# Rotary embedding on one core: loads and stores from two DMA queues, or from one queue in a written order

## The chip, the core and the metric

The kernel runs on one core of a Trainium2 chip. The metric is device time in microseconds, the median of three runs. A profiled execution gives the trace from which all other times here come.

## The reference

```
x: (8, 2048, 16, 64) float32; cos, sin: (2048, 32) float32
x1, x2 = x[..., :32], x[..., 32:]
out1 = x1 * cos - x2 * sin        # cos, sin per sequence position,
out2 = x1 * sin + x2 * cos        # the same for all batches and heads
out  = concat([out1, out2], -1)
```

Each element is read once and written once: 67.1 MB in, 67.1 MB out, three vector operations on each.

## The kernel before

A batch's 2048 positions lie on 128 partitions, 16 consecutive positions on each. A piece is half of that: 8 positions, 128 partitions x 8192 floats, 4 MB. There are 16 pieces, and `buf` has room for 5 of them; piece p uses place p mod 5, is rotated in place and is stored from there. So the load of piece p + 5 has to wait until piece p is stored.

At the start SyncE issues the two tables and the first piece in three parts (L101 to L105), then pieces 1 to 4 (L106, `load` at L52). ScalarE copies the tables into PSUM (`sin_p` with both signs, `cos_p`; L108 to L110). ScalarE then does nothing but issue stores (`store` at L55).

`rotate` works on half a piece (4 positions, 128 x 4096). VectorE multiplies the half-swapped piece by sin into `v` (L80) and the piece by cos in place (L93); GpSimd adds `v` to it (L99). `v` has two buffers, so VectorE can be at most two halves ahead of GpSimd. In piece 15 a part of the adds stays on VectorE, with `w` in PSUM (L87, L96), and the store is cut in three. The order of VectorE's work is pinned by `in_order`.

Loads are in SyncE's DMA queue, stores in ScalarE's; each queue is in order in itself. When both have work, packets of 32 KB (one partition's row of a piece) from the two alternate on each of the 16 DMA engines. Nothing ties the order of one queue to that of the other except the data: a store waits for GpSimd (and VectorE in piece 15), a load for the store that frees its place, the arithmetic for its load. Below, load 5 and store 5 are short for those of piece 5.

Of the kernel before, what the change touches and what calls it, by code (L numbers as in the profile page):

```python
# [1 line left out]

# [4 lines left out]


@with_exitstack  # L10
def kernel(
    ctx: ExitStack,
    tc: tile.TileContext,
    x: bass.AP,
    cos: bass.AP,
    sin: bass.AP,
    out: bass.AP,
):
    nc = tc.nc
    f32 = mybir.dt.float32  # L20

    B, S, H, D = x.shape
    Dh = D // 2
    P = nc.NUM_PARTITIONS
    J = S // P
    R = 8
    C = 4
    HALVES = J // R
    NP = B * HALVES
    NBUF = 5  # L30

    const_pool = ctx.enter_context(tc.tile_pool(name="rope_const", bufs=1))
    io_pool = ctx.enter_context(tc.tile_pool(name="rope_io", bufs=1))
    tmp_pool = ctx.enter_context(tc.tile_pool(name="rope_tmp", bufs=2))
    ps_pool = ctx.enter_context(tc.tile_pool(name="rope_ps", bufs=1, space=bass.MemoryType.PSUM))
    psv_pool = ctx.enter_context(tc.tile_pool(name="rope_psv", bufs=1, space=bass.MemoryType.PSUM))

    sin_f = const_pool.tile([P, J, Dh], f32)
    cos_f = const_pool.tile([P, J, Dh], f32)
    sin_p = ps_pool.tile([P, J, D], f32)  # L40
    cos_p = ps_pool.tile([P, J, Dh], f32)
    buf = io_pool.tile([P, NBUF, R, H, D], f32)

    def rows(t, p, r0, r1):
        b, j0 = p // HALVES, (p % HALVES) * R
        return t[b].rearrange("(p j) h d -> p j (h d)", j=J)[:, j0 + r0 : j0 + r1, :].rearrange("p j f -> p (j f)")

    def flat(t):
        return t.rearrange("p j h d -> p (j h d)")

    def load(p, r0=0, r1=R):
        nc.sync.dma_start(out=flat(buf[:, p % NBUF, r0:r1, :, :]), in_=rows(x, p, r0, r1))  # L52

    def store(p, r0=0, r1=R):
        nc.scalar.dma_start(out=rows(out, p, r0, r1), in_=flat(buf[:, p % NBUF, r0:r1, :, :]))  # L55

    order = []

    def in_order(op):
        if order:  # L60
            tc.add_manual_dep(
                op.ins,
                order[-1].ins.name,
                mybir.DependencyInfo(mybir.DependencyClass.NoSync, mybir.DependencyReason.DATA),
                reason="order of the vector engine",
            )
        order.append(op)

    def rotate(p, r0, r1, on_vector=0):
        n = r1 - r0  # L70
        j0 = (p % HALVES) * R + r0
        js = slice(j0, j0 + n)
        xt = buf[:, p % NBUF, r0:r1, :, :]
        rev = xt.rearrange("p j h (e d) -> p j h e d", e=2)[:, :, :, ::-1, :]
        sin_b = sin_p[:, js, :].rearrange("p j (e d) -> p j e d", e=2).unsqueeze(2).to_broadcast([P, n, H, 2, Dh])
        cos_b = cos_p[:, js, :].unsqueeze(2).to_broadcast([P, n, 2 * H, Dh])
        m = n - on_vector
        if m:
            v = tmp_pool.tile([P, C, H, D], f32)
            in_order(nc.vector.tensor_mul(  # L80
                out=v[:, 0:m, :, :].rearrange("p j h (e d) -> p j h e d", e=2),
                in0=rev[:, 0:m, :, :, :],
                in1=sin_b[:, 0:m, :, :, :],
            ))
        if on_vector:
            w = psv_pool.tile([P, 2, H, D], f32)
            in_order(nc.vector.tensor_mul(  # L87
                out=w[:, 0:on_vector, :, :].rearrange("p j h (e d) -> p j h e d", e=2),
                in0=rev[:, m:n, :, :, :],
                in1=sin_b[:, m:n, :, :, :],  # L90
            ))
        xw = xt.rearrange("p j h (e d) -> p j (h e) d", d=Dh)
        in_order(nc.vector.tensor_mul(out=xw, in0=xw, in1=cos_b))  # L93
        if on_vector:
            xa = flat(xt[:, m:n, :, :])
            in_order(nc.vector.tensor_add(out=xa, in0=xa, in1=flat(w[:, 0:on_vector, :, :])))  # L96
        if m:
            xa = flat(xt[:, 0:m, :, :])
            nc.gpsimd.tensor_add(out=xa, in0=xa, in1=flat(v[:, 0:m, :, :]))  # L99

    nc.sync.dma_start(out=sin_f, in_=sin.rearrange("(p j) d -> p j d", j=J))  # L101
    load(0, 0, 2)
    nc.sync.dma_start(out=cos_f, in_=cos.rearrange("(p j) d -> p j d", j=J))
    load(0, 2, 4)
    load(0, 4, R)  # L105
    for p in range(1, NBUF):  # L106
        load(p)
    nc.scalar.copy(out=sin_p[:, :, Dh:D], in_=sin_f)  # L108
    nc.scalar.mul(out=sin_p[:, :, 0:Dh], in_=sin_f, mul=-1.0)  # L109
    nc.scalar.copy(out=cos_p, in_=cos_f)  # L110
    for p in range(NP):
        if p == 0:
            rotate(p, 0, 2)
            rotate(p, 2, 4)
            rotate(p, 4, 8)
            store(p)
        elif p == NP - 1:
            rotate(p, 0, 4, 1)
            store(p, 0, 4)
            rotate(p, 4, 6, 1)  # L120
            store(p, 4, 6)
            rotate(p, 6, 8, 2)
            store(p, 6, 8)
        else:
            rotate(p, 0, 4)
            rotate(p, 4, 8)
            store(p)
        if p + NBUF < NP:
            load(p + NBUF)


# [1 line left out]
_INS = ['x', 'cos', 'sin']  # L133
_OUTS = [((8, 2048, 16, 64), 'float32')]


# [23 lines left out]
```

## Time and profile before

| | |
|---|---|
| median of 3 runs | 318.86 us (318.46 to 319.0) |
| the profiled execution | 318.49 us, of which the span is 316.7 us |
| VectorE busy | 287.5 us (91%), 73 instructions |
| GpSimd busy | 274.8 us (87%), 37 instructions |
| ScalarE busy | 3.1 us |
| loads, queue 1 | 67.63 MB, 50.0% of the 16 DMA engines' span |
| stores, queue 10 | 67.11 MB, 49.1% |
| a 4 MB load or store, issue to landing | 31.4 us (median) |

An engine's busy time is what it spends in instructions; issuing a DMA isn't counted. The DMA share of a slice or a window is the mean over 16 engines. A packet's bytes are counted where the packet starts, so a short window that cuts a burst shows more or less than what flows.

### The profile page before, as it was taken

The page shows a single profiled execution, that of the slowest core. Times are in us where ns is not written, and L with a number is a line of the kernel's source. Part 1 is how long each engine was busy: PE and PEld are TensorE (multiplying, and loading weights), DVE is VectorE, ACT ScalarE, POOL GpSimd, SP SyncE. Part 2 cuts the span into 40 slices and gives each one's busy share as a digit, 9 for nine tenths or more (in the row PEclk, how much of TensorE's full clock was granted, in tenths as well). Part 3 has the DMA queues.
Part 4 walks back from the last instruction along what each step waited for, and adds up shares of the span by engine and source line. Part 5 has one row for each costly group of instructions (what it writes and reads, how often), then busy time and mean ns, then how long its engine had stood idle before and what let it go on. Part 6 is the DMA issues. An engine that isn't in the chain of part 4 may idle for free.

```text
span 316.7 us, 272 instructions
## 1 busy us (share of the span) xinstructions
DVE 287.5 (91%) x73; ACT 3.1 (1%) x4; POOL 274.8 (87%) x37
## 2 busy tenths in 40 slices
DVE  2999999999999999999999999799697997979960
ACT  3000000000000000000000000000000000000000
POOL 0659999999999999999999999989969899797900
DMA  7999999999999999999999999999999999999997
GB/s 301 460 430 447 348 464 426 435 451 410 459 401 464 397 464 397 464 414 447 435 426 459 401 464 397 464 398 459 410 451 435 426 451 410 455 406 460 406 428 300
DMA packets 5474, 134.76 MB, mean 425 GB/s; under 512 B 608, under 2 KB 608, under 8 KB 864
## 3 DMA queue, kind: packets, MB, share of 16 engines
q1 hardware_dynamic: 2880, 67.63, 50.0%
q10 hardware_dynamic: 2592, 67.11, 49.1%
q14 instruction: 2, 0.02, 0.0%
HBM read 67.63 MB, written 67.11 MB: 425 GB/s over the span
## 4 chain that ended last, share of the span: by engine, by line
POOL 39%; DMA 32%; DVE 21%; issue 3%; SPq 0%; POOLq 0%; DVEq 0%
POOL buf L99 39%; DMA buf<-in_x_dram 22%; DMA out_dram<-buf 11%; DVE buf L93 10%; DVE v L80 8%; DVE buf L96 1%; DVE w L87 1%; SPq L101 0%; POOLq L99 0%; DVEq L80 0%; SPq L52 0%
## 5 line engine op out<-in xcount | busy, mean ns | idle before, releaser
L99 POOL TENSOR_TENSOR buf<-buf,v 128x4096 f32<-128x4096 f32 (+3 forms) x33 | 274.6, 8335 | 26.2 <-DVE buf L93 25.8
L80 DVE TENSOR_TENSOR v<-buf,sin_p 128x4096 f32<-128x4096 f32 (+3 forms) x33 | 137.3, 4161 | 17.3 <-DMA buf<-in_x_dram 15.7
L93 DVE TENSOR_TENSOR buf<-buf,cos_p 128x4096 f32<-128x4096 f32 (+1 forms) x34 | 141.8, 4170 | 1.2
L96 DVE TENSOR_TENSOR buf<-buf,w 128x1024 f32<-128x1024 f32 (+1 forms) x3 | 4.7, 1575 | 0.1
L87 DVE TENSOR_TENSOR w<-buf,sin_p 128x1024 f32<-128x1024 f32 (+1 forms) x3 | 4.7, 1579 | 0.0
L108 ACT ACT_TABLE_LOAD x1 | 1.3, 1283 | 0.7 <-PEq L144 0.7
L110 ACT COPY cos_p<-cos_f 128x512 f32<-128x512 f32 x1 | 0.6, 590 | 2.1 <-DMA cos_f<-in_cos_dram 2.1
L108 ACT COPY sin_p<-sin_f 128x512 f32<-128x512 f32 x1 | 0.6, 589 | 1.4 <-DMA sin_f<-in_sin_dram 1.4
L109 ACT ACTIVATE sin_p<-sin_f 128x512 f32<-128x512 f32 x1 | 0.6, 601 | 0.0
L144 POOL MEMSET const-float32-0.0<- 128x1 f32 x1 | 0.1, 98 | 0.2 <-issue 0.2
L144 POOL MEMSET const-bfloat16-1.0<- 128x1 bf16 x1 | 0.1, 101 | 0.0
L144 POOL MEMSET const-uint8-127<- 128x1 uint8 x1 | 0.1, 101 | 0.0
L144 POOL MEMSET const-float32-1.0<- 128x1 f32 x1 | 0.1, 98 | 0.0
## 6 DMA issues: line engine op xcount, KB each, us to landing
buf<-in_x_dram SPq DMA_DIRECT2D x15, 4096.0 KB, 31.4
out_dram<-buf ACTq DMA_DIRECT2D x15, 4096.0 KB, 31.4
buf<-in_x_dram SPq DMA_DIRECT2D x2, 1024.0 KB, 6.0
buf<-in_x_dram SPq DMA_DIRECT2D x1, 2048.0 KB, 11.5
out_dram<-buf ACTq DMA_DIRECT2D x1, 2048.0 KB, 11.9
out_dram<-buf ACTq DMA_DIRECT2D x2, 1024.0 KB, 10.8
sin_f<-in_sin_dram SPq DMA_DIRECT2D x1, 256.0 KB, 2.7
cos_f<-in_cos_dram SPq DMA_DIRECT2D x1, 256.0 KB, 5.1
```

The lines of the kernel that those rows point to most:

```text
L80: in_order(nc.vector.tensor_mul(out=v[:, 0:m, :, :].rearrange("p j h (e d) -> p j h e d", e=2), in0=rev[:, 0:m, :, :, :], in1=sin_b[:, 0:m ...
L87: in_order(nc.vector.tensor_mul(out=w[:, 0:on_vector, :, :].rearrange("p j h (e d) -> p j h e d", e=2), in0=rev[:, m:n, :, :, :], in1=sin_ ...
L93: in_order(nc.vector.tensor_mul(out=xw, in0=xw, in1=cos_b))
L96: in_order(nc.vector.tensor_add(out=xa, in0=xa, in1=flat(w[:, 0:on_vector, :, :])))
L99: nc.gpsimd.tensor_add(out=xa, in0=xa, in1=flat(v[:, 0:m, :, :]))
L108: nc.scalar.copy(out=sin_p[:, :, Dh:D], in_=sin_f)
L109: nc.scalar.mul(out=sin_p[:, :, 0:Dh], in_=sin_f, mul=-1.0)
L110: nc.scalar.copy(out=cos_p, in_=cos_f)
L144: nc = _bacc.Bacc("TRN2", target_bir_lowering=False, num_devices=1)
```

## The change

All DMAs, tables, loads and stores, are issued by SyncE, and each is tied to the one before it (`in_ring`), so that the queue's order is that of the program. The order is: the tables and piece 0 in three parts, loads 1 to 4, stores 0 and 1, load 5, store 2, load 6, store 3, and so on to load 15, store 12, then stores 13, 14 and the three parts of 15. The first store is a whole piece as before. In the instruction order of the built program VectorE and GpSimd have the same instructions in the same order as before, ScalarE has no DMA any more, and SyncE has the 38 DMAs in the order above.

```
+    def in_ring(dma):
+        if ring:
+            tc.add_manual_dep(dma.ins, ring[-1].ins.name, ...)
+        ring.append(dma)
+
     def load(p, r0=0, r1=R):
-        nc.sync.dma_start(out=flat(buf[...]), in_=rows(x, p, r0, r1))
+        in_ring(nc.sync.dma_start(out=flat(buf[...]), in_=rows(x, p, r0, r1)))

     def store(p, r0=0, r1=R):
-        nc.scalar.dma_start(out=rows(out, p, r0, r1), in_=flat(buf[...]))
+        in_ring(nc.sync.dma_start(out=rows(out, p, r0, r1), in_=flat(buf[...])))
...
     load(0, 4, R)
-    for p in range(1, NBUF):
-        load(p)
+    load(1)
+    load(2)
...
+    rotate(0, 0, 2)
+    load(3)
+    load(4)
+    rotate(0, 2, 4)
+    rotate(0, 4, 8)
+    store(0)
+    rotate(1, 0, 4)
+    rotate(1, 4, 8)
+    store(1)
+    for p in range(2, NP - 1):
+        if p + 3 < NP:
+            load(p + 3)
+        rotate(p, 0, 4)
+        rotate(p, 4, 8)
+        store(p)
+    p = NP - 1
+    rotate(p, 0, 4, 1)
+    store(p, 0, 4)
+    rotate(p, 4, 6, 1)
+    store(p, 4, 6)
+    rotate(p, 6, 8, 2)
+    store(p, 6, 8)
```

## The prediction

> **What bounds the kernel now.** I read the page's rows of DMA share and GB/s first, since engines at 91% and 87% could bind as well; then the chain, the waits, and the DMA share by windows.
>
> ```profile
> DMA  7999999999999999999999999999999999999997
> GB/s 301 460 430 447 348 464 426 435 451 410 459 401 464 397 464 397 464 414 447 435 426 459 401 464 397 464 398 459 410 451 435 426 451 410 455 406 460 406 428 300
> DMA packets 5474, 134.76 MB, mean 425 GB/s; under 512 B 608, under 2 KB 608, under 8 KB 864
> ```
>
> All 16 DMA engines are full from the second slice to the last but one, so transfers are the limit from end to end. The GB/s swing because a slice holds whole bursts of 32 KB packets. Windows cut where bursts begin remove that:
>
> ```profile
> 25.40:35.10 9.70, 9.47 (x3) 0.00 (x0) 9.70 (x2) 1.00 1.00 432
> 35.10:38.40 3.30, 3.27 (x2) 0.00 (x0) 3.30 (x1) 1.00 1.01 328
> 38.40:48.10 9.70, 9.66 (x3) 0.00 (x0) 9.54 (x2) 1.00 1.01 436
> 48.10:57.80 9.70, 9.51 (x3) 0.00 (x0) 9.70 (x2) 1.00 1.00 432
> 314.00:315.00 1.00, 0.00 (x0) 0.00 (x0) 0.00 (x0) 1.00 0.45 188
> 315.00:316.70 1.70, 0.00 (x0) 0.00 (x0) 0.00 (x0) 1.00 0.01 5
> ```
>
> The last two columns are DMA share and GB/s. Loads alone run at 432 (row 1, which holds a boundary between two loads, at 33 us). Loads and stores from two queues, packet by packet, run at 436 and 432 (rows 3, 4). So direction and mixture make no difference, with one exception: row 2, just after the first store is issued at 33.31. The engines are full there, yet move only 328: two load packets per engine take 1.53 and 1.70 us on average in the packet records, where every packet before and after takes 1.213. Loss: 3.27 us from the first of these to the first store packet, less 2 x 1.213 = 0.84 us. I call it the dip. No other window shows one. The last rows show the tail: by 315.0 one engine of 16 still works, about half a microsecond after most.
>
> Compute is close behind, but not the limit:
>
> ```profile
> SPq L52 <- DMA out_dram<-buf: 240.7, 11, 50.2
> ...
> DVE v L80 <- DMA buf<-in_x_dram: 15.7, 7, 6.1
> ...
> 60.13 53.46 POOL L99 TENSOR_TENSOR buf<-buf,v 128x4096 f32<-128x4096 f32 x6 [0.16 <-DVE buf L93]
> ...
> 283.16 3.35 DVE L80 TENSOR_TENSOR v<-buf,sin_p 128x3072 f32<-128x3072 f32 x1 [1.68 <-DMA buf<-in_x_dram]
> ...
> 303.89 2.29 DVE L96 TENSOR_TENSOR buf<-buf,w 128x2048 f32<-128x2048 f32 x1
> ```
>
> Columns of the waits: total us, times, longest. All 11 later loads wait for a store to clear their buffer. GpSimd's six adds in 53.46 us make 8.91 each; two halves make a piece in 17.8 to 17.9 us. A piece in and out is 8.39 MB, 19.4 us at 432 GB/s. So VectorE ends up waiting for loads. The last piece starts at 283.16 and its arithmetic ends at 306.2, 9.3 us before the last packet (315.5): compute is off the end.
>
> **The change part by part.** *The profiled execution* took 318.49 us: 1.8 to the first packet, 313.7 of packets, 1.2 after the last, and 1.8 outside the span (316.7). The median of the runs shown is 318.86, 0.37 above it.
>
> *Bytes, packets, arithmetic.* The same, in the same order on each compute engine. The 313.7 us can only fall by the dip and the uneven tail, and rise by holes in the queue.
>
> *18 stores move from ScalarE's issue to SyncE's.* A store issue takes 0.34 us, 18 x 0.34 = 6.1 us on an engine that mostly waits. Nothing queues behind them on ScalarE, whose work ends at 7.3 us. Price 0, under full DMA engines. Without that cover each would delay one transfer by 0.34 us.
>
> *SyncE's fixed order.* Now a store that waits for its arithmetic holds every load behind it, and a load that waits for a buffer holds the stores behind it. With Lp and Sp for the load and the store of piece p, SP's order after L4 is S0 S1 L5 S2 L6 S3 and so on to L15 S12 S13 S14, then S15 in three parts. I lay it on the rates above, 9.71 us per 4 MB transfer. Loads 0 to 4 (20.97 MB and the tables) fill the queue to 52.5. Then S0 runs to 62.2, S1 to 71.9, L5 to 81.6, S2 to 91.3, and each further load and store add 19.4: L15 lands at 275.8, S12 ends at 285.5, S13 295.2, S14 304.9, S15 314.6. Against that:
> - S0's arithmetic is ready at 33.3, 19 us before its slot; S1's at 51.2 (the store issue in the trace), 11 before; S2's at 69.0, 12.6 before. Later ones come every 17.9 against 19.4, so the margin grows until the tail.
> - L5 needs S0 landed (62.2), and its slot is 71.9; L6 needs S1 (71.9), slot 91.3. After that each load's buffer is free a load and a store ahead. From issue to first packet takes 1.05 us at the start (0.74 to 1.79), and 5.1 for the first store, of which 3.3 were packets ahead of it. The smallest margin, 9.7 us, covers both.
> - Tail: piece 15 starts at 275.8 instead of 283.16 and ends 23.0 later (306.2 - 283.2), at 298.8; its last part has its slot at 312.2. S14 is ready near 284, slot 295.2.
>
> So the queue never empties, VectorE's 15.7 us of waiting for loads shrinks to some 7 (the head's 6.1 and little more), and that saving is worth nothing, since the transfers set the end. Price 0.
>
> *The first store behind five loads.* The new queue makes one load-to-store step at 52.5 instead of opening a second queue at 33.3. Whether the dip belongs to the second queue or to the step itself, the trace of before can't say: it has both once, at one time. Bounds: from -0.84 (dip gone) to 0 (dip moves). Later steps between loads and stores inside one queue (12 from load to store, 11 back) appear nowhere in before. Nearest rows: 0 for a step of direction between two queues (rows 3, 4) and for a boundary of equal direction in one queue (row 1); 0.84 for the dip. I take 0: both halves of such a step are in the trace at no cost, and the mixed windows contain a step at every packet.
>
> *The uneven tail.* One engine ends some 0.5 us after most. Bounds -0.5 to +0.5 us, as the late engine isn't tied to the queues; I take 0.
>
> Sum: 318.49 - 0.84 = 317.65 on the profiled execution; on the scale of the median 318.86 - 0.84, 318.0 us.
>
> *A rule that speaks against it.* The Trainium skill, "DMA: Bandwidth & Descriptors", section "Anatomy of one DMA — SWDGE (gpsimd) path", fits about 2.0 us of fixed time per DMA beside its bytes, for transfers of another issuing path. If one queue paid that between all its 38 transfers, the estimate by this page would be some 70 us more. Row 1 disagrees: a boundary in one queue lies inside it at 432 GB/s, so it gets no chance of its own.
>
> **The rivals.**
>
> *The dip only moves.* It belongs to the first store, not to the queue. For: stores are new at that moment as well. Against: it is spent in load packets, before the first store packet begins. Time: 318.5 on the profiled execution, 318.9 on the median; 0.5 less if the tail evens out. The Trainium skill, "DMA: Bandwidth & Descriptors", section "Issuing engines are not separate DMA queues", says that transfers run on the same 16 engines whoever issues them, and that another issuer saves only issue time. By that rule nothing changes; rows 1 and 4 agree with it, row 2 is open.
>
> *The dip comes back at each step (slower).* A block of loads turning into a block of stores costs something each time, as the engines must end one direction before the other flows; in before, interleaved packets hide it after the first time. Place: the starts of S0, S2, S3 up to S12, 12 steps. At the dip's full price 12 x 0.84 - 0.84 = +9.2, 327.7 us; at 0.25 each +2.2, 320.7. It decides from (0.64 + 0.84) / 12 = 0.12 us per step. Against: rows 3 and 4. For: the only load-to-store step of a pure stream that the trace has did cost 0.84.
>
> *A store holds the loads behind it (slower).* If GpSimd's cadence slips, or a landing is told late, SP waits and the engines run dry. It decides when a margin of 9.7 us is used up; one such hole of 2 us gives 320.5. Against: GpSimd's cadence is steady, and margins grow.
>
> **How the numbers follow.** About 0.2%, 0.64 us, is what a measurement of this kernel can tell from no change. The forecast, dip gone, has 0.50; its 0.84 us is only just beyond that, so 0.45 faster and 0.05 same. The dip that moves has 0.27: 0.22 same, 0.03 faster through the tail, 0.02 slower. The dip at each step has 0.18, a held queue 0.05, both slower. Faster 0.48, same 0.27, slower 0.25. Range: down to 316.9 (dip and uneven tail both gone: 318.49 - 0.84 - 0.5 = 317.15, less 0.25 as half the spread of the runs), up to 320.6 (a step price of 0.25 us); the dearer steps and holes are left out.
>
> **What would show it.** Right: one queue carries 134.7 MB at 432 GB/s through windows across the first load-to-store step near 52.5 us and across later ones; no slices below "9" in the DMA row but the first and the last; piece 15 starts near 276; the last packet is near 314.6. The dip moved: one window near 50 to 53 at some 330 GB/s. Dip at each step: windows of 19.4 us below 432 throughout, and VectorE waiting for loads late in the run. Held queue: a DMA slice of "8" or less in the middle, with SP waiting for GpSimd. The forecast is wrong if the time is above 318.5, or if the time falls without any change near the first store.

## The result, and the profile after

The changed kernel takes 322.8 us (median of 5 runs, 321.87 to 323.43) against 318.66 us for the kernel before: a ratio of 1.0127, 95% interval 1.0108 to 1.0146. It is slower by 4.1 us, where 0.84 us faster was forecast as likeliest. The profiled execution took 322.37 us, with a span of 320.6.

The page of the changed kernel, DMA share and rates in 40 slices, and the queues:

```profile
DMA  8999999999999999999999999999999999999994
GB/s 304 469 405 458 413 437 393 421 429 458 405 442 421 429 442 413 437 429 429 429 421 433 446 413 442 439 425 433 417 442 433 429 429 429 446 422 429 433 412 177
q1 hardware_dynamic: 5472, 134.74, 98.4%
```

The DMA engines are never empty in the middle: the fixed order holds nothing up. What stands out is the last slice, 177 GB/s instead of 300. Windows of the changed kernel, cut around the first store and over the tail (last columns: DMA share, GB/s):

```profile
49.60:52.90 3.30, 3.14 (x2) 0.00 (x0) 3.30 (x2) 1.00 1.03 328
52.90:62.50 9.60, 9.57 (x3) 0.00 (x0) 9.44 (x2) 1.00 1.00 433
313.00:315.00 2.00, 0.00 (x0) 0.00 (x0) 0.00 (x0) 1.00 0.98 414
315.00:316.00 1.00, 0.00 (x0) 0.00 (x0) 0.00 (x0) 1.00 0.49 205
316.00:317.00 1.00, 0.00 (x0) 0.00 (x0) 0.00 (x0) 1.00 0.29 123
317.00:318.00 1.00, 0.00 (x0) 0.00 (x0) 0.00 (x0) 1.00 0.12 49
318.00:319.40 1.40, 0.00 (x0) 0.00 (x0) 0.00 (x0) 1.00 0.06 23
```

The dip is there again, in the last two packets of load 4, now ahead of the store at 53 us, with the same 328 GB/s in a window of the same length. And the tail is long: from 315 us on the share falls by steps to 0.06, one engine of 16. Before, 0.01 was left after 315.0. The last of the 16 DMA engines is done at 319.3, 1.3 us before the span ends; the first is done at 315.0.

Where the engines come apart can be read from the ends of the transfers on each engine, in the packet records (us):

| end of | first engine | last engine | apart |
|---|---|---|---|
| load 4 | 52.94 | 53.42 | 0.48 |
| store 1 | 72.30 | 72.78 | 0.48 |
| load 5 | 82.01 | 82.83 | 0.82 |
| load 6 | 101.43 | 102.86 | 1.43 |
| load 7 | 120.92 | 123.04 | 2.11 |
| load 8 | 140.29 | 143.40 | 3.10 |
| load 12 | 218.07 | 222.00 | 3.93 |
| load 15 | 276.16 | 280.51 | 4.35 |
| the last store | 315.01 | 319.32 | 4.31 |

Each full store adds 9.68 us to the first and to the last engine alike: 62.62 to 72.30 and 63.10 to 72.78 for store 1, and so through the run. Nearly every loss is in the last packets of a load that has a store behind it. There the first engine pays 0.54 us in all over loads 5 to 15, and the last one 0.37 to 1.00 us at seven of the eleven, 4.4 us together. No late engine comes back.

The waits of the changed kernel, first those of SyncE's queue, then VectorE's (total us, times, longest):

```profile
SPq L67 <- POOL buf L111: 142.7, 14, 27.2
SPq L64 <- DMA out_dram<-buf: 136.7, 11, 19.2
```

```profile
DVE v L92 <- DMA buf<-in_x_dram: 12.9, 5, 6.2
```

SyncE waits for GpSimd 14 times, 142.7 us in all, and no DMA slice shows it: this waiting is ahead of need. VectorE still waits 12.9 us for loads, and what it waits for is the last engine's part of a load: piece 15 starts at 280.90, 0.4 us after the last engine ends load 15 and 4.7 after the first. Its line:

```profile
280.90 3.35 DVE L92 TENSOR_TENSOR v<-buf,sin_p 128x3072 f32<-128x3072 f32 x1 [1.76 <-DMA buf<-in_x_dram]
```

### The profile page after: what moved, and what is told of

Read it like the earlier page. It is cut to its first block, busy times and chain, and to the rows that moved or that the text cites. A ratio compares the mean times of both kernels' runs of the same rounds, so it can differ in the third digit from the quotient of the medians.

```text
span 320.6 us, 261 instructions
## 1 busy us (share of the span) xinstructions
DVE 287.5 (90%) x73; ACT 3.1 (1%) x4; POOL 274.8 (86%) x37
## 4 chain that ended last, share of the span: by engine, by line
POOL 36%; DMA 34%; DVE 21%; issue 3%; SPq 0%; POOLq 0%; DVEq 0%
POOL buf L111 36%; DMA out_dram<-buf 23%; DMA buf<-in_x_dram 11%; DVE buf L105 10%; DVE v L92 8%; DVE buf L108 1%; DVE w L99 1%; SPq L113 0%; SPq L64 0%; POOLq L111 0%; DVEq L92 0%; SPq L67 0%
## 5 line engine op out<-in xcount | busy, mean ns | idle before, releaser
L92 DVE TENSOR_TENSOR v<-buf,sin_p 128x4096 f32<-128x4096 f32 (+3 forms) x33 | 137.3, 4162 | 15.0 <-DMA buf<-in_x_dram 12.9
```

Of the source, the lines that this page charges most:

```text
L92: in_order(nc.vector.tensor_mul(out=v[:, 0:m, :, :].rearrange("p j h (e d) -> p j h e d", e=2), in0=rev[:, 0:m, :, :, :], in1=sin_b[:, 0:m ...
```

## The experiments

Theories after the result. *Step:* each step from a block of loads to a block of stores delays some engines' last load packets, at a price that does not depend on how the blocks are cut. *Queue:* one queue for everything lets the engines drift, whatever the order. *Block:* the price needs a long block of one direction; a short one is free, in one queue as in two. *Cold start:* only the first store costs something.

**Two loads, two stores.** Fewer steps, longer blocks.

```
+        if p % 2 == 0:
+            for l in (p + 3, p + 4): load(l)      # then store(p), store(p + 1)
```

> One queue as in the changed kernel, but after store 1 two loads and two stores in turn: 7 steps from load to store instead of 12, the same packets and arithmetic. Step theory (each step from a block of loads to a block of stores delays the last load packets of the DMA engines that trail; the first step costs all of them): the 4.1 us that the changed kernel loses come from its 11 steps after the first, so 6 such steps cost about 2.2 us: some 320.9 us, and the engines end some 2.5 us apart instead of 4.3. Queue theory (engines drift apart because one queue carries everything, whatever the order): no change, 322.8 us. Cold-start theory (the loss is the first store's alone): no change, 322.8 us.

Measured 321.0 us, ratio 1.0088 (1.0071 to 1.0105) to the kernel before: 2.6 us lost instead of 4.1. The last engine ends 1.7 us after the first, 317.26 against 315.57. The time is the step theory's 320.9; the engines end 1.7 us apart where it had 2.5. The queue and the cold start allow no change. Per step after the first the median loses 2.6 / 6 = 0.43 us, against 4.1 / 11 = 0.37: a block of twice the length costs about the same.

**Halves and eighths by partitions.** Meant to double the steps, and to alternate packet by packet, with unchanged packets.

```
+        for k in range(K):            # K = 2, 8
+            load(p + 3, k=k)          # partitions k, k + K, ...
+            store(p, k=k)
```

> One queue, but from load 5 to store 12 each transfer is cut in two by partitions (even, odd), and half loads and half stores alternate: 23 steps from load to store instead of 12, packets of 32 KB as before, 4 instead of 8 per engine and step. Step theory: the loss doubles, 318.7 + 8.2 = about 327 us. Queue theory: 322.8 us. Block theory (the price is of long blocks of one direction and grows with their length): less than 322.8, about 320.7 us.

> One queue, from load 5 to store 12 cut in eight by partitions, so that each DMA engine has one 32 KB packet of a load, then one of a store, and so on: the same alternation that two queues give, written into one queue, with 89 steps from load to store. Step theory with a price per step: far slower, 318.7 + 8 x 4.1 = about 351 us. Queue theory: 322.8 us or more. Block theory: as the kernel before, 318.7 us within 1 us.

Measured 567.64 and 711.12 us, and these totals say nothing on the theories. The split by partitions gave loads a wait for arithmetic on another piece, which whole pieces don't have. The halves' DMA row, and the two longest waits of their SyncE queue:

```profile
DMA  9999995383382391490590690771762752840658
```

```profile
SPq L69 <- DVE buf L113: 296.6, 10, 32.8
SPq L75 <- POOL buf L119: 196.7, 17, 38.0
```

Loads wait 296.6 us for VectorE, and in the one queue everything behind them waits too. This is the third rival of the prediction, the held queue, in pure form: it shows in the DMA row at once, and it isn't what the changed kernel does.

Up to the first of these waits, near 95 us, the DMA engines are full, and that stretch does bear on the theories. In the eighths by partitions it holds load 5 and store 2, one packet of 32 KB in each direction by turns. Their window, and behind it the kernel before in the same stretch, where two queues alternate by packets of 32 KB (last columns: DMA share, GB/s):

```profile
72.40:94.40 22.00, 0.00 (x0) 0.00 (x0) 0.00 (x0) 1.00 1.02 338
```

```profile
72.40:94.40 22.00, 21.76 (x6) 0.00 (x0) 21.86 (x3) 1.00 1.01 438
```

All engines are full in both, and the one queue moves 338 GB/s instead of 438. In its packet records a load packet takes 1.72 us there on average and a store packet 1.40, instead of 1.213, with no gap between them: 0.7 us for each step to a store and back, while VectorE and GpSimd do nothing. So a block of 0.5 MB is not free in one queue, where the block theory had "as the kernel before". The halves by partitions make two steps before their waits. These cost the average engine 0.16 and 0.18 us, and loads 5 and 6 of the changed kernel cost it 0.15 each: half the block, about the same price.

**The first store early.** Is the dip the first store's, or that of any step out of pure loads?

```
     load(1)
+    store(0, 0, 2)      # 1 MB, behind load 1; then loads 2 to 4
...
-    store(0)
+    store(0, 2, 8)
```

> One queue as in the changed kernel, but the first quarter of piece 0 is stored on its own behind load 1, so that the first store starts near 23.5 us and the first long block of stores near 55 us. If the dip is the first store's alone (something that happens once): a dip of 0.8 to 1.0 us on every engine in load 1, just before 23.5 us, and nothing for the leading engine before the second store; total 322.8 us. If the dip is the price of a step out of a long pure block of loads: 0.8 us or more before both stores, total 323.6 us.

Measured 322.17 us (ratio 1.0121, 1.0102 to 1.0141). Windows of this kernel around the early store and around the end of load 4, where the second store begins:

```profile
21.80:24.80 3.00, 2.56 (x1) 0.00 (x0) 0.35 (x1) 1.00 0.82 240
...
46.10:55.90 9.80, 9.77 (x3) 0.00 (x0) 9.64 (x2) 1.00 1.01 437
```

The dip has moved with the first store to the end of load 1, where it costs the first engine 1.2 us (10.89 instead of 9.68) and the average engine 1.4. Ahead of the second store, after three pure loads, nothing is lost: the first and the last engine take 9.68 us for load 4. So in a stream without pauses the dip comes once, with the first store, in ScalarE's queue (before) as in SyncE's. After pauses it can come again: in the halves by partitions, whose engines run empty for some 15 us in each of ten pieces, the second half load of each of these pieces takes the average engine 1.1 to 1.35 us more than its packets' usual time. The early store also shows a step out of 12.6 MB of loads that costs nothing while the engines are 0.66 us apart; the later steps cost as usual.

**Halves and eighths by rows, in one queue and in two.** The cut that leaves the waits alone, with its controls. It also makes the packets shorter: 16 KB in halves, 4 KB in eighths.

```
+        for r in range(0, R, n):      # n = 4: halves; n = 1: eighths
+            load(p + 3, r, r + n)
+            store(p, r, r + n)        # one: nc.sync; two: nc.scalar
```

> One queue; from load 5 to store 12 each transfer is cut in two by rows (positions 0 to 3, 4 to 7 of a piece) and half loads and half stores alternate: 23 steps from load to store instead of 12, packets of 16 KB there. Packet overhead: 0.611 against 1.213 / 2 us, 88 packets a DMA engine more than half as long, 0.8 us in all. Step theory (a price per step for engines that trail): about 318.7 + 0.8 + 8.2 = 327.7 us. Queue theory (one queue, whatever the order): 323.6 us. Block theory (the price belongs to long blocks of one direction): under 322 us.

> The control: the same halves and the same program order, with the stores in ScalarE's queue. All theories: 318.6 + 0.8 = about 319.4 us, engines less than 1 us apart at the end.

> One queue; from load 5 to store 12 each transfer is cut in eight by rows, so that 512 KB of loads and 512 KB of stores alternate, 1.2 us each, at the pace at which two queues alternate by packets of 32 KB; 89 steps from load to store. Packets are 4 KB there and cost more: an engine's 8 KB packet takes 0.309 us, 2% over its share of 1.213; for 4 KB that gives some 4%, about 8 us on the 92 MB concerned, which the control shares. Step theory: 33 us over the control. Queue theory: 4 us over the control. Block theory: as the control.

> The control for the eighths: the same cuts and program order, with the stores in ScalarE's queue. All theories: 318.6 us and the price of 4 KB packets, about 8 us: 326 to 327 us.

| | one queue | two queues | difference |
|---|---|---|---|
| halves, 2 MB blocks, 23 steps | 322.52 us (1.0100 to 1.0146) | 319.9 us (1.0030 to 1.0064) | 2.6 us |
| eighths, 0.5 MB blocks, 89 steps | 326.02 us (1.0207 to 1.0249) | 326.26 us (1.0202 to 1.0268) | -0.2 us |

In brackets the intervals of the ratio to the kernel before. The tails, halves in one queue and in two, then eighths in one and in two:

```profile
316.00:317.00 1.00, 0.00 (x0) 0.00 (x0) 0.00 (x0) 1.00 0.63 262
317.00:319.20 2.20, 0.00 (x0) 0.00 (x0) 0.00 (x0) 1.00 0.25 104
```

```profile
316.00:317.00 1.00, 0.00 (x0) 0.00 (x0) 0.00 (x0) 1.00 0.14 57
317.00:319.20 2.20, 0.00 (x0) 0.00 (x0) 0.00 (x0) 1.00 0.00 0
```

```profile
321.00:322.00 1.00, 0.00 (x0) 0.00 (x0) 0.00 (x0) 1.00 0.45 188
322.00:324.00 2.00, 0.00 (x0) 0.00 (x0) 0.00 (x0) 1.00 0.02 8
```

```profile
321.00:322.00 1.00, 0.00 (x0) 0.00 (x0) 0.00 (x0) 1.00 0.85 360
322.00:324.00 2.00, 0.00 (x0) 0.00 (x0) 0.00 (x0) 1.00 0.08 33
```

With eighths by rows the one queue ends as evenly as two queues, and as early: the queue theory falls. Twice the steps of half the length cost less than the changed kernel, 2.6 us and not 8.2: a price per step that is the same for every cut falls too.

The block theory would fit these rows: per step 0.37 us for blocks of 4 MB, 2.6 / 22 = 0.12 us for 2 MB, nothing to be seen for 0.5 MB. It doesn't fit the eighths by partitions, which have the same number of transfers, the same blocks of 0.5 MB and the same order in one queue. In the stretch shown there, the eighths by rows move, in one queue and then in two:

```profile
72.40:94.40 22.00, 21.76 (x6) 0.00 (x0) 21.85 (x3) 1.00 1.02 417
```

```profile
72.40:94.40 22.00, 21.75 (x6) 0.00 (x0) 21.84 (x3) 1.00 1.00 411
```

One queue is no slower here than two, and every load packet of load 5 takes its usual 0.159 us. What differs from the eighths by partitions (338 GB/s) is the cut, and with it the packets: 4 KB against 32. Ordered by packets, the runs agree: at 32 KB a step costs 0.43 us in blocks of 8 MB, 0.37 in blocks of 4 MB, and more rather than less in blocks of 0.5 MB; at 16 KB it costs 0.12, at 4 KB nothing to be seen. So the price goes with the packets or with the way of cutting, not with the block. This reading came out of the runs, and none of them was built for it: no run changes the length of the packets alone, so which of the two it is stays open.

**Without the arithmetic.** Does it need VectorE and GpSimd beside the transfers?

```
     def rotate(p, r0, r1, on_vector=0):
+        return
```

> The changed kernel with the rotation left out (VectorE's and GpSimd's work, x is only copied): the same 38 transfers in the same order in one queue. If the price of the steps needs the engines' own traffic to the buffers beside the transfers, it goes: 318.7 us, only the dip, engines within 1 us at the end. If it belongs to the transfers alone: about 322 us, engines some 4 us apart.

> The control: the kernel before with the rotation left out, loads and stores in two queues. Both theories: 318 to 319 us with the dip, which should come near 15 us, where the first store can now start.

Measured 321.72 us in one queue (ratio 1.0086, 1.0059 to 1.0113) and 318.64 us in two (0.9997, 0.9967 to 1.0026). The tails, one queue first (no VectorE column, as it does nothing):

```profile
315.00:317.00 2.00, 0.00 (x0) 0.00 (x0) 1.00 0.35 147
317.00:319.40 2.40, 0.00 (x0) 0.00 (x0) 1.00 0.09 38
```

```profile
315.00:317.00 2.00, 0.00 (x0) 0.00 (x0) 1.00 0.04 16
317.00:319.40 2.40, 0.00 (x0) 0.00 (x0) 1.00 0.00 0
```

3.1 us are lost between them, with engines 3.4 us apart in the one queue. The transfers alone suffice for most of the loss; whether the rest of the 4.1 us needs the arithmetic, the intervals (1.0086 here, 1.0127 with it) don't settle. In two queues the arithmetic's own time is worth nothing. Their dip, expected near 15 us, lies at 15.6 to 19.0 us, again ahead of the first store.

**A small first write.** Can the dip be taken at the start, beside the wait for the first load?

```
+    first = const_pool.tile([P, 128], f32)
+    nc.vector.memset(first, 0.0)
+    nc.scalar.dma_start(out=rows(out, NP - 1, 7, 8)[:, 0:128], in_=first)
```

> The kernel before with one small store more, ahead of everything in ScalarE's queue: 128 x 128 zeros into the last rows of the output, which the last store writes again later. The early store of 1 MB showed that the dip comes once, with the first store. If a small store is enough and its wait lies beside the start (first load packet at 1.8 us): no dip near 35 us, 318.5 - 0.8 = 317.7 us. If the dip needs a full stream of loads, or many stored bytes: it stays at 35 us, 318.5 us. If the cost only moves to the head: no dip at 35, but the first loads land 0.8 us later, 318.5 us.

Measured 318.6 us, ratio 0.9991 (0.9971 to 1.001). The dip stays where it was:

```profile
25.50:35.10 9.60, 9.37 (x3) 0.00 (x0) 9.60 (x2) 1.00 1.00 430
35.10:38.50 3.40, 3.37 (x2) 0.00 (x0) 3.40 (x1) 1.00 0.96 308
```

So 64 KB stored early do not spend it; the 1 MB of the early store did. What it is stays open, and no version here beats the kernel before.

**The blocks in two queues.**

```
+        if r1 - r0 == R:
+            return (("sync", 0, 4), ("scalar", 4, 8))   # a half of each load and store in each queue
```

> The changed kernel's order of blocks in two queues: from the second half of piece 0 on, SyncE's queue carries one half of each load and store (positions 0 to 3) and ScalarE's the other (4 to 7), both in the order load 5, store 2, load 6, store 3 and so on, so that two queues alternate by packets but the direction still changes only every 4 MB. Packets of 16 KB cost about 1.1 us more on all pieces; two queues are never exactly in step, and some packets of the two directions will mix around each step. If the price comes from long blocks of one direction: some 322 us, DMA engines 3 to 4 us apart at the end. If it comes from a load and a store following each other in one queue: about 319.9 us as with halves in two queues, engines within 1 us.

Eleven executions run from 319.65 to 328.9 us: five below 320.2, one at 322.88, five above 326. Without those five the ratio is 1.0058 (1.0028 to 1.0088), some 320.4 us, between the two expectations. The trace, of an execution of 326.66 us, shows why this doesn't test what it was meant to: the halves of store 0 end on their first engines at 59.0 us in SyncE's queue and at 65.8 in ScalarE's. The queues are 6.8 us out of step in blocks of 9.7, so loads of one run beside stores of the other for most of the time. At the end its engines are 7.6 us apart, so two queues alone don't hold the engines together. Whether steps cost the same in two queues that keep step stays open.

## Why the prediction was wrong

**The step that failed** is "Later steps between loads and stores inside one queue", for which I took 0. They cost 4.1 us on the median, 0.37 each. (There are 11 of them from load to store; the 12 of the prediction include the first.) The reason I gave was that "the mixed windows contain a step at every packet": I took the alternation of two queues for steps inside one. The eighths by partitions put that alternation, with the same packets of 32 KB, into one queue, and it moves 338 GB/s there instead of 438. A step inside one queue was free only with the 4 KB packets of the eighths by rows. Of the two ends given, 0 and 0.84, the value lay near the middle. Why a step inside one queue costs anything stays open.

**The uneven tail**, taken at 0 with bounds of half a microsecond, is the place where that price appears: 4.3 us between first and last engine, 1.0 before. The sum had one time for the DMA engines. With 16 of them, each in order by itself, the end is set by the last. The first ended at 315.0, beside 314.6 in the prediction, and that agreement is partly luck: the dip was still there, and 27 transfers at 9.68 us instead of the 9.71 of the prediction gave about as much back.

**The dip** did not go (-0.84 forecast, 0): the window at 49.6 moves the same 328 GB/s, and the early store shows it belongs to the first store. The rival "the dip only moves" was right on this term. That it lies in load packets spoke against this rival in the prediction; the last load packets ahead of a store are just where nearly all losses of the changed kernel lie.

**The rival "the dip comes back at each step"** has the right sign and place; at 0.37 us, far over its threshold of 0.12, it was given 0.18. Its reason, that the engines must end one direction before the other flows, is not shown by any run. Its price is mis-sized: a step costs the first engine next to nothing and the last up to 1.0, and later steps pay less than the first store does. It looked for the loss in windows "below 432 throughout"; the changed kernel's windows from 120.8 to 140.5 and from 181.5 to 201 us move 434 and 432, and the loss shows in the spread between engines. My range was cut at 0.25 us a step.

**Right:** SyncE's fixed order costs nothing by itself. The margins held, no slice is below 9 in the middle, and the 142.7 us for which stores wait for GpSimd are covered. The dispatch of 18 stores by SyncE is not seen. VectorE's wait for loads, forecast at some 7 us, came at 12.9. The doubt about 2 us of fixed time per transfer in the Trainium skill, "DMA: Bandwidth & Descriptors", section "Anatomy of one DMA — SWDGE (gpsimd) path", was justified: no such time stands between queued transfers here, as consecutive 4 MB stores end 9.68 us apart, which is their packets' own time. Piece 15 was forecast at 275.8 and came at 280.9; both misses are the late engines again, as load 15 landed at 280.5.

The other rule, of "Issuing engines are not separate DMA queues" in the same page of the Trainium skill, leads to no change. The eighths by rows agree with it (-0.2 us between one queue and two); the changed kernel doesn't, by 4.1 us, and in the eighths by partitions one queue moved 338 GB/s where the two queues of the kernel before moved 438.

## What to carry to other kernels

With all DMA engines full, moving the issue of stores changed nothing here through issue time or waits, but it decided whether loads and stores flow side by side from two queues or one behind the other in one. Look at the end of the profile for a share that falls in steps, which means engines that have come apart. Two queues mixed loads and stores here at full rate without any planning. In one queue a step from loads to stores cost some 0.4 us with packets of 32 KB, in blocks of 4 MB as of 8, and 32 KB packets that took turns one by one cost almost a quarter of the rate (338 against 438 GB/s). With 4 KB packets one queue was as good as two, though cutting by rows into them cost 7.5 us (326.0 against 318.5) by itself. A stage that looks identical in every mean rate (432 GB/s in windows of both kernels) can still lose time in the spread between engines, so price a step by its slowest engine, and not by a window's mean. And a run that misses its aim may still hold a stretch that answers the question: read it up to where it goes wrong.

## What was not expected of the hardware

- At a step from 4 MB of loads to 4 MB of stores in one queue, an engine's last load packet takes up to 2.2 us instead of 1.213, on some engines only, and at some steps hardly at all (loads 10, 11, 13 and 15 on the last engine). Store packets and the other load packets keep 1.213 with few exceptions. Why these engines and these steps is open.
- Single packets of 32 KB, a load and a store by turns, take 1.72 and 1.40 us in one queue and 1.213 from two. By turns of eight 4 KB packets one queue costs nothing.
- The first bulk of stores costs the average engine 0.8 to 1.4 us, in the load packets ahead of it, whether in its own queue or in a shared one. A first store of 64 KB doesn't. In a stream without pauses this comes once; where the engines had run empty in between, it came again.
